# Four groups of the MLP's first layer by seven products, single modulation steps, and a schedule with other costs, in a fused hybrid block

## The chip, the core and the metric

One core of a Trainium2 chip runs the whole program. The metric is the device time of one execution in microseconds (us); the median of three runs of the kernel before is 822.44.

## What is computed

One decoder layer on x (512 tokens x 1024, fp32), with a conditioning vector c. The reference, cut to what matters here:

```python
mod = silu(c) @ w_ada + b_ada
shift1, scale1, gate1, shift2, scale2, gate2 = split(mod, 6)
h = rms_norm(x, g_pre_mix) * (1 + scale1) + shift1
z = h @ w_in                                     # GLU input | q latent | kv latent | rotary key | gates
u = silu(layer_norm(causal_depthwise_conv(ua * sigmoid(ub)), conv_norm_g, conv_norm_b))
y_a = u @ w_conv_out                             # branch A
q  = rms_norm(q_lat, q_norm_g) @ w_uq            # branch B: attention over low-rank latents
kv = rms_norm(kv_lat, kv_norm_g) @ w_ukv
y_b = softmax attention(q, kv, rope) @ w_attn_out
x = x + gate1 * rms_norm((sigmoid(g_a) * y_a + sigmoid(g_b) * y_b) @ w_out, g_post_mix)
h = rms_norm(x, g_pre_mlp) * (1 + scale2) + shift2
y = square(relu(h @ w_mlp_in)) @ w_mlp_out       # 1024 -> 4096 -> 1024
x = x + gate2 * rms_norm(y, g_post_mlp)
```

## The kernel before, in words

**Arithmetic.** Every fp32 matrix product is made of three products of the type fp32r, which rounds: `mm3` (L454) multiplies high by high, high by low and low by high part into the same PSUM bank. A high part is a ScalarE cast, a low part a VectorE subtraction (`W`, L475, for weights; `split`, L459). "A product" below is one instruction on TensorE: 128 x 128 weights times 128 x 512 (or x 256) columns.

**Who sets the order.** The program isn't issued as it is written. `Planner` (L164 to 390) records every operation with the region it reads and writes (`record`, L245; `region`, L195), gives it a cost (`cost`, L217), works back from TensorE's order when each must be done, and lists each engine's instructions by that (`plan`, L306): TensorE in the order of writing, the others by due time less a bonus (`plan.hurry`). `Arena` and `Banks` hand out places in two SBUF arenas (`f_arena` for fp32, `r_arena` for fp32r) and in PSUM. The whole is repeated `PASSES` times, each with the lifetimes of the pass before, and the pass with the shortest planned length is issued (L385), so that every instruction in the trace has the line L388. Tiles are told apart by their names: `f_arena`, `r_arena`, `psum`, `mod`, `lns` (layer norm's statistics), `stats` (those of the RMS norms).

**The front.** The tokens are loaded, normalized and transposed. The shift and scale of the first norm come from `w_ada`; they are needed as columns, one for each 128 channels. `ada_load` (L522) loads the rows of one column pair or of several, VectorE multiplies them by c and adds them up (L705 to 709), `to_columns` (L640) sums over partitions on TensorE with a vector of ones, and `first_products` (L652) forms h for these 128 channels and starts 21 products with `w_in`. The loop over `KGRP` (L694) takes channels 2 and 3 together, 4 and 5 together, then 6 and 7 singly.

**The middle.** The rest of the input projection, the latents' norm (`lat_norm`, L867), attention with the convolution spread beside it, `layer_norm` (L1233, over channels, with statistics broadcast by TensorE from diagonal matrices), the output projections and the gates.

**The MLP.** Its 4096 hidden channels are worked in four chunks (`for ch in range(NCH)`, L1527), each of eight tiles of 128 channels. A chunk's first layer takes 8 x 8 x 3 = 192 products of 512 columns (for the first four tiles of chunk 0 twice as many of 256, because the second half of the tokens comes later). The second layer (`strassen`, L1447) multiplies 2 x 2 blocks with seven products instead of eight, the sums of blocks being made by VectorE: 7 x 24 = 168 products of 512 columns. `add_block` (L1565) adds them to the result, and in the last chunk does the last norm and the output.

The core of a seven-product scheme, as it stands in the second layer:

```python
b_sub(t1, b12, b11)
b_sub(t2, b22, t1)
dve.tensor_tensor(a3(s1), A(1, 0), A(1, 1), ALU.add)
dve.tensor_tensor(a3(s2), a3(s1), A(0, 0), ALU.subtract)
product(a_form(a3(s2)), b_form(t2), ba, False)
banked(0, 1, ba)
```

The fourth argument of `product` says whether the bank is begun anew; with `False` the product is added onto what `banked` has just read out.

## Time and profile before

| | |
|---|---|
| runs | 822.37, 822.44, 826.56 us (median 822.44) |
| the profiled execution | 821.15 us; its span 819.4 us |
| TensorE busy | 799.6 us (98%), 3934 instructions, clock 0.997 of full speed |
| VectorE busy | 685.5 us (84%) |
| ScalarE busy | 423.3 us (52%) |
| GpSimd busy | 28.5 us (3%) |
| moved by DMA | 117.28 MB, mean 143 GB/s |

The span runs from the first to the last instruction of the profiled execution; its time has 1.75 us around that. Busy times are sums over the whole span and hide that the stages have different limits; the rows further down are taken by stretch.

### The profile page before, as it was taken

What the parts mean: (1) busy time and instruction counts of PE and PEld (TensorE: products, weight loads), DVE (VectorE), ACT (ScalarE), POOL (GpSimd) and SP (SyncE); (2) the same over time, 40 slices, a digit from 0 to 9 for tenths busy, and PEclk for the clock granted to TensorE, in tenths of its full rate; (3) what the DMA queues carried; (4) which work ended last, traced back from release to release, by engine and by line L of the source; (5) the groups of instructions that cost most, each with busy time, mean ns of one, the idle gap of its engine ahead of it and who ended that gap; (6) DMA issues with size and microseconds to landing.
All of it is one profiled execution on the core that took longest, in us unless ns stands there. A gap on an engine that the chain in (4) does not pass through costs nothing.

```text
span 819.4 us, 10628 instructions
## 1 busy us (share of the span) xinstructions
PE 799.6 (98%) x3934; PEld 673.5 (82%) x3934; DVE 685.5 (84%) x1014; ACT 423.3 (52%) x714; POOL 28.5 (3%) x84
## 2 busy tenths in 40 slices
PE   6999999999999999999999989999999999999995
PEld 4778988899988888888888889888888888888884
DVE  4989899999999999989999798397539993975696
ACT  5373554375894255228334496465345434553552
POOL 2001210000000000000000020000000000000001
PEclk9999999999999999999999999999999999999998
DMA  9997324202263151134799660173015831660302
GB/s 305 330 336 256 126 76 122 80 1 77 79 206 103 27 154 52 52 98 154 255 325 385 239 188 26 52 227 108 0 52 165 283 117 52 201 209 1 103 0 104
DMA packets 87111, 117.28 MB, mean 143 GB/s; under 512 B 7345, under 2 KB 61970, under 8 KB 87058
## 3 DMA queue, kind: packets, MB, share of 16 engines
q1 hardware_dynamic: 87058, 116.59, 44.1%
q8 instruction: 31, 0.51, 0.3%
q14 instruction: 22, 0.18, 0.1%
HBM read 108.18 MB, written 8.39 MB: 142 GB/s over the span
## 4 chain that ended last, share of the span: by engine, by line
PE 95%; ACT 2%; DVE 1%; POOL 1%; DMA 0%; issue 0%; DVEq 0%; ACTq 0%
PE psum L388 95%; DVE f_arena L388 1%; ACT f_arena L388 1%; POOL stats L388 1%; ACT r_arena L388 0%; DMA f_arena<-in_x_dram 0%; ACT stats L388 0%; DVEq L1639 0%; DVE mod L388 0%; ACTq L388 0%
## 5 line engine op out<-in xcount | busy, mean ns | idle before, releaser
L388 PE MATMUL psum<-r_arena 128*128 128x512 f32 (+2 forms) x3592 | 761.5, 372 | 3.2 <-ACT r_arena L388 3.1
L388 PEld LDWEIGHTS psum<-r_arena 128*128 128x128 f32 x3592 | 632.5, 188 | 114.8 <-ACT r_arena L388 3.8
L388 DVE TENSOR_TENSOR r_arena<-f_arena,r_arena 128x1024 fp32r<-128x1024 f32 (+4 forms) x234 | 247.7, 1081 | 92.1 <-PE psum L388 57.6
L388 ACT CAST r_arena<-f_arena 128x1024 fp32r<-128x1024 f32 (+4 forms) x224 | 210.2, 959 | 179.4 <-PE psum L388 117.8
L388 DVE SCALAR_TENSOR_TENSOR f_arena<-f_arena,cw 128x512 f32<-128x512 f32 x240 | 164.9, 744 | 0.0
L388 ACT ACTIVATE f_arena<-psum 128x512 f32<-128x512 f32 x64 | 38.1, 597 | 120.0 <-PE psum L388 119.8
L388 DVE TENSOR_TENSOR f_arena<-f_arena 128x1024 f32<-128x1024 f32 (+3 forms) x78 | 77.0, 1003 | 5.8 <-ACT f_arena L388 3.6
L388 ACT ACTIVATE f_arena<-f_arena 128x512 f32<-128x512 f32 (+4 forms) x100 | 58.5, 604 | 18.6 <-DVE f_arena L388 17.4
L388 DVE SCALAR_TENSOR_TENSOR f_arena<-f_arena,cT 128x256 f32<-128x256 f32 (+2 forms) x84 | 55.3, 699 | 0.1
L388 PE MATMUL psum<-ident,f_arena 128*128 128x128 f32 x234 | 34.9, 286 | 7.6 <-DVE f_arena L388 7.6
L388 PEld LDWEIGHTS psum<-ident,f_arena 128*128 128x128 f32 x234 | 28.8, 147 | 13.0 <-DVE f_arena L388 8.4
L388 DVE TENSOR_TENSOR f_arena<-psum,f_arena 128x512 f32<-128x512 f32 x52 | 35.5, 684 | 4.6 <-PE psum L388 4.4
L388 DVE TENSOR_TENSOR r_arena<-psum,r_arena 128x512 fp32r<-128x512 f32 (+2 forms) x57 | 35.7, 656 | 1.7 <-ACT r_arena L388 1.0
L388 POOL TENSOR_TENSOR stats<-stats,nhalf 128x1 f32<-128x1 f32 x24 | 20.1, 842 | 476.2 <-ACT stats L388 476.2
L388 ACT CAST r_arena<-psum 128x512 fp32r<-128x512 f32 (+2 forms) x57 | 30.1, 566 | 11.1 <-PE psum L388 10.7
L388 ACT COPY f_arena<-psum 128x512 f32<-128x512 f32 (+5 forms) x42 | 19.8, 500 | 17.6 <-PE psum L388 17.6
L388 ACT ACTIVATE r_arena<-f_arena 128x512 fp32r<-128x512 f32 (+3 forms) x20 | 13.0, 651 | 18.3 <-DVE f_arena L388 16.0
L388 DVE CUSTOM_DVE_ANT_0 f_arena<-psum,mask 128x128 f32<-128x128 f32 (+3 forms) x32 | 15.2, 485 | 2.7 <-PE psum L388 2.5
L388 ACT ACTIVATE f_arena<-f_arena,lnh 128x512 f32<-128x512 f32 x16 | 12.2, 808 | 6.8 <-DVE f_arena L388 6.7
L388 DVE TENSOR_SCALAR f_arena<-f_arena,stats 128x1024 f32<-128x1024 f32 x8 | 6.0, 751 | 10.5 <-POOL stats L388 10.5
L388 DVE SCALAR_TENSOR_TENSOR f_arena<-f_arena 128x512 f32<-128x512 f32 (+1 forms) x18 | 13.2, 743 | 0.2 <-ACT f_arena L388 0.2
L388 DVE SCALAR_TENSOR_TENSOR f_arena<-f_arena,psum 128x512 f32<-128x512 f32 x16 | 10.7, 679 | 0.0
(94 smaller groups left out, 180.3 us busy)
## 6 DMA issues: line engine op xcount, KB each, us to landing
f_arena<-in_w_ada_dram SPq DMA_DIRECT2D x16, 1024.0 KB, 5.3
f_arena<-in_w_mlp_in_dram SPq DMA_DIRECT2D x32, 512.0 KB, 4.4
f_arena<-in_w_mlp_out_dram SPq DMA_DIRECT2D x32, 512.0 KB, 5.4
f_arena<-in_w_in_dram SPq DMA_DIRECT2D x24, 512.0 KB, 4.1
f_arena<-in_x_dram SPq DMA_DIRECT2D x8, 512.0 KB, 5.4
f_arena<-in_w_ada_dram SPq DMA_DIRECT2D x16, 256.0 KB, 5.6
f_arena<-in_w_ada_dram SPq DMA_DIRECT2D x8, 512.0 KB, 7.1
h_spill<-r_arena SPq DMA_DIRECT2D x16, 256.0 KB, 3.8
```

Source lines behind the costliest of these rows:

```text
L388: getattr(self.real[o.eng], o.fn)(*o.a, **o.k)
```

## The change

1. **First MLP layer.** Four groups of four hidden tiles, `SIN` = (chunk, first tile) (0, 4), (1, 0), (1, 4), (2, 4), are worked with seven products of blocks instead of eight. A group is a product of a 512 x 1024 by a 1024 x 512 matrix; in 2 x 2 blocks a block product is 24 products of 256 columns, so 7 x 24 = 168 of 256 columns take the place of 96 of 512. `h2_sums` makes four sums of activation blocks once, `strassen_in` a group. The fp32 activations are kept for it (`h2f`, 4096 words of a partition).
2. **Front.** `KGRP` has single steps; shift and scale are summed by one VectorE instruction of 256 elements instead of two; within a step, the 21 products go by kind of part (all high by high, then high by low, then low by high). Ten small loads (six vectors, the positions, three of the convolution's weights), which stood ahead of the first step, come behind the last modulation load.
3. **`lat_norm`** takes the roots of all four token tiles in one instruction instead of eight, after all squares and before all scalings.
4. **The planner's costs** are others (a product of 256 columns, a load by the length of its pieces, a queue of eight loads, a delay for GpSimd), and 14 passes are made. So the order of instructions changes everywhere.

The diff, cut to its core (`run` gives the length in bytes of a load's contiguous pieces; `region` takes DRAM by offset):

```diff
@@ -44,10 +44,13 @@
-PASSES = 8
+SIN = ((0, 4), (1, 0), (1, 4), (2, 4))
+DEPTH = 8
+PASSES = 14
 LEAD = 15000.0
+SLOW = 4000.0
 ADAS = (1, 1, 0, 4)
-KGRP = ((2, 3), (4, 5), (6,), (7,))
+KGRP = ((2,), (3,), (4,), (5,), (6,), (7,))
...
@@ -218,17 +235,17 @@
         if fn == "dma_start":
-            return 475.0, 2000.0
+            return 375.0, 2000.0
...
-                return max(53.5, n / 2.4 + 2) * 4, 190.0
-            return max(64.0, n / 2.4 + 2.5), 190.0
+                return (213.0 if n == 1 else max(53.5, n / 2.4 + 2) * 4), 190.0
+            return max(109.0, n / 2.4 + 13.3), 190.0
...
-            o.dma = b
+            n = min(self.run(outs[0]), self.run(ins[0]), 4096)
+            o.dma = b * (13.0 + 0.0385 * n) / (16 * n)
...
                     if o.dma:
                         st = max(now + 1100.0, dma_free)
-                        dma_free = st + o.dma / 360.0
-                        o.t1 = dma_free + 910.0
+                        dma_free = st + o.dma
+                        o.t1 = dma_free + 1100.0
+                        landed.append(o.t1)
+                        free[e] = max(free[e], landed[-DEPTH])
...
@@ -660,9 +677,12 @@
-            for i in range(NA + NB):
-                o = i // 2 if i % 2 == 0 else NA + i // 2
-                mm3(pb.v(g1b[i]), w(0, o * P, P), hs(k), k == 0, k == KD - 1)
+
+            for wi, hi in ((0, 0), (0, 1), (1, 0)):
+                for i in range(NA + NB):
+                    o = i // 2 if i % 2 == 0 else NA + i // 2
+                    pe.matmul(pb.v(g1b[i]), lhsT=w(0, o * P, P)[wi], rhs=hs(k)[hi], start=k == 0 and wi + hi == 0,
+                              stop=k == KD - 1 and wi == 1)
...
             for j in range(KD):
-                for s in range(2):
-                    if j == 0:
-                        dve.tensor_scalar(accv[:, s], av[:, s, 0], cT[:, 0:1], None, ALU.mult)
-                    else:
-                        dve.scalar_tensor_tensor(accv[:, s], av[:, s, j], cT[:, j:j + 1], accv[:, s], op0=ALU.mult, op1=ALU.add)
+                if j == 0:
+                    dve.tensor_scalar(accv, av[:, :, 0], cT[:, 0:1], None, ALU.mult)
+                else:
+                    dve.scalar_tensor_tensor(accv, av[:, :, j], cT[:, j:j + 1], accv, op0=ALU.mult, op1=ALU.add)
...
@@ -719,6 +739,17 @@
+        plan.after = ada_end
+        row_loads(1, ("gpl", g_pre_mlp), ("cb", conv_b), ("cng", conv_norm_g), ("cnb", conv_norm_b),
+                  ("qg", q_norm_g), ("kvg", kv_norm_g))
+        sp.dma_start(out=pos4, in_=positions[0].rearrange("(a p) -> a p", p=P))
...
+            sp.dma_start(out=fa.v(cwr)[at:at + r1 - r0, c0:c0 + P], in_=cw_rows[r0:r1])
+        plan.after = None
...
@@ -865,16 +896,19 @@
-                rstd(s[:, 2:3], s[:, 0:1], 1.0 / QL)
-                rstd(s[:, 3:4], s[:, 1:2], 1.0 / KL)
...
+            rstd(s[:, 2 * NT:], s[:, :2 * NT], 1.0)
...
@@ -1524,11 +1561,110 @@
+        def h2_sums():
+
+            Y = {(j, i): k4(fa.v(h2f[j]))[:, :, 256 * i:256 * i + 256] for j in range(2) for i in range(2)}
+            for nm, o, a, b in ((3, (0, 1), (1, 1), (0, 1)), (1, (0, 0), None, (0, 0)), (2, (1, 1), (1, 1), (0, 0)),
+                                (4, (1, 0), (1, 0), (1, 1))):
+                if nm == 1:
+
+                    dve.tensor_tensor(Y[0, 0], Y[1, 1], Y[0, 0], ALU.subtract)
+                    dve.tensor_tensor(Y[0, 0], Y[0, 0], Y[0, 1], ALU.subtract)
+                else:
+                    dve.tensor_tensor(Y[o], Y[a], Y[b], ALU.subtract)
+                hl = pair(1024)
+                act.copy(k4(ra.v(hl[0])), Y[o])
+                dve.tensor_tensor(k4(ra.v(hl[1])), Y[o], k4(rf(hl[0])), ALU.subtract)
+                h2s_[nm] = hl
+            fa.free(*h2f)
+
+        def strassen_in(hv, n0, c0):
...
+            def product(xb, y, b, first):
+                w = W(fa.v(xb, "p (k n) -> p k n", k=4), 4, 256)
...
+                for m in range(2):
+                    for k in range(4):
+                        mm3(pb.v(b)[:, m * 256:(m + 1) * 256], w(k, m * P, P), ys_[k], first and m == 0 and k == 0, k == 3,
+                            skip_group_check=True)
+                w.free()
...
+            def keep(i, n, b):
+                act.copy(o(i, n), ps(b))
+
+            def done(i, n, b):
+                v = o(i, n)
+                dve.tensor_tensor(v, ps(b), v, ALU.add)
+                act.activation(v, v, AF.Relu)
+                act.activation(v, v, AF.Square)
+
+            x11, x12 = x_(0, 0), x_(0, 1)
+            ba, bb, bc_ = (pb.alloc() for _ in range(3))
+            product(x11, (0, 0), ba, True)
+            keep(0, 0, ba)
+            product(x12, (1, 0), bc_, True)
+            done(0, 0, bc_)
+            pb.free(bc_)
+            x21, x22 = x_(1, 0), x_(1, 1)
+            s1, s2 = fa.alloc(1024), fa.alloc(1024)
+            sub(s1, x21, x22, ALU.add)
+            sub(s2, s1, x11)
+            product(s2, 2, ba, False)
+            keep(0, 1, ba)
+            product(s1, 1, bb, True)
+            fa.free(s1)
+            keep(1, 1, bb)
+            sub(x21, x11, x21)
+            fa.free(x11)
+            product(x21, 3, ba, False)
+            fa.free(x21)
+            done(1, 1, ba)
+            sub(x12, x12, s2)
+            fa.free(s2)
+            product(x12, (1, 1), bb, False)
+            fa.free(x12)
+            done(0, 1, bb)
+            pb.free(bb)
+            product(x22, 4, ba, False)
...
             for n0 in range(0, HPC, GRP):
+                if (ch, n0 - n0 % 4) in SIN:
+                    if n0 % 4 == 0:
+                        if not h2s_:
+                            h2_sums()
+                        strassen_in(hv, n0, (ch * HPC + n0) * P)
...
+                    continue
```

How the order moves, at the three places that the prediction speaks of. In these rows `x` with a number counts equal instructions in a row.

TensorE in the MLP, from the last transposes into it to the end, before (`ident` marks a transpose, `onesr` a broadcast of the last gate):

```order
L388 MATMUL psum<-ident,f_arena 128x128 x12
L388 MATMUL psum<-r_arena 128x512 x11
L388 MATMUL psum<-r_arena 128x256 x6
L388 MATMUL psum<-ident,f_arena 128x128 x4
L388 MATMUL psum<-r_arena 128x256 x63
L388 MATMUL psum<-ident,f_arena 128x128 x12
L388 MATMUL psum<-r_arena 128x256 x123
L388 MATMUL psum<-r_arena 128x512 x1176
L388 MATMUL psum<-r_arena,onesr 128x512 x4
L388 MATMUL psum<-r_arena 128x512 x168
```

and now:

```order
L410 MATMUL psum<-ident,f_arena 128x128 x12
L410 MATMUL psum<-r_arena 128x512 x17
L410 MATMUL psum<-r_arena 128x256 x24
L410 MATMUL psum<-ident,f_arena 128x128 x4
L410 MATMUL psum<-r_arena 128x256 x53
L410 MATMUL psum<-ident,f_arena 128x128 x12
L410 MATMUL psum<-r_arena 128x256 x283
L410 MATMUL psum<-r_arena 128x512 x168
L410 MATMUL psum<-r_arena 128x256 x336
L410 MATMUL psum<-r_arena 128x512 x264
L410 MATMUL psum<-r_arena 128x256 x168
L410 MATMUL psum<-r_arena 128x512 x360
L410 MATMUL psum<-r_arena,onesr 128x512 x4
L410 MATMUL psum<-r_arena 128x512 x168
```

In all 384 products of 512 columns have gone and 672 of 256 have come, in three pieces; ahead of the first four transposes stand 17 + 24 products instead of 11 + 6.

TensorE in the front, from the first modulation column to the last (`ones` 128x1 is the sum over partitions for a shift and a scale), before:

```order
L388 MATMUL psum<-ones,f_arena 128x1 x2
L388 MATMUL psum<-r_arena 128x512 x49
L388 MATMUL psum<-ones,f_arena 128x1 x2
L388 MATMUL psum<-r_arena 128x512 x8
L388 MATMUL psum<-ones,f_arena 128x1 x2
L388 MATMUL psum<-r_arena 128x512 x9
L388 MATMUL psum<-ones,f_arena 128x1 x2
L388 MATMUL psum<-r_arena 128x512 x20
L388 MATMUL psum<-ones,f_arena 128x1
L388 MATMUL psum<-r_arena 128x512
L388 MATMUL psum<-ones,f_arena 128x1
L388 MATMUL psum<-r_arena 128x512 x54
```

and now:

```order
L410 MATMUL psum<-ones,f_arena 128x1 x2
L410 MATMUL psum<-r_arena 128x512 x23
L410 MATMUL psum<-ones,f_arena 128x1 x2
L410 MATMUL psum<-r_arena 128x512 x22
L410 MATMUL psum<-ones,f_arena 128x1 x2
L410 MATMUL psum<-r_arena 128x512 x21
L410 MATMUL psum<-ones,f_arena 128x1 x2
L410 MATMUL psum<-r_arena 128x512 x21
L410 MATMUL psum<-ones,f_arena 128x1 x2
L410 MATMUL psum<-r_arena 128x512 x21
L410 MATMUL psum<-ones,f_arena 128x1 x2
L410 MATMUL psum<-r_arena 128x512 x27
```

The sums of the pair (4, 5), the two instructions x2 after x49 and after x8, and those of 6 and 7 are now asked for one by one, 21 to 23 products apart.

VectorE at the layer norm, from the last token tile's statistics to the diagonals (`lns` 128x4 are the small sums, 128x512 the additions of convolution taps), before:

```order
L388 TENSOR_TENSOR lns<-lns 128x4
L388 SCALAR_TENSOR_TENSOR f_arena<-f_arena 128x512
L388 TENSOR_SCALAR lns<-lns 128x4
L388 TENSOR_TENSOR lns<-lns 128x4
L388 SCALAR_TENSOR_TENSOR f_arena<-f_arena 128x512
L388 TENSOR_SCALAR lns<-lns 128x4
L388 TENSOR_TENSOR lns<-lns 128x4 x2
L388 SCALAR_TENSOR_TENSOR f_arena<-f_arena 128x512
L388 TENSOR_TENSOR lns<-lns 128x4
L388 SCALAR_TENSOR_TENSOR f_arena<-f_arena 128x512
L388 TENSOR_SCALAR f_arena<-f_arena,cT 128x1024
L388 TENSOR_SCALAR f_arena<-ident,lns 128x128
L388 TENSOR_TENSOR lns<-lns 128x4
L388 TENSOR_SCALAR f_arena<-ident,lns 128x128 x3
```

and now:

```order
L410 TENSOR_TENSOR lns<-lns 128x4
L410 SCALAR_TENSOR_TENSOR f_arena<-f_arena 128x512
L410 TENSOR_SCALAR lns<-lns 128x4
L410 TENSOR_TENSOR lns<-lns 128x4 x2
L410 TENSOR_SCALAR lns<-lns 128x4
L410 TENSOR_TENSOR lns<-lns 128x4 x2
L410 TENSOR_SCALAR f_arena<-ident,lns 128x128
L410 TENSOR_TENSOR lns<-lns 128x4
L410 TENSOR_SCALAR f_arena<-ident,lns 128x128 x3
```

One addition of 512 elements stands among the small sums instead of four, and one of 1024 ahead of the first diagonal is gone. On TensorE the broadcast (`f_arena,ones`) had 27 products of 512 columns ahead of it since the last transposes, and has 16 now.

## Rows read from the trace of the kernel before

**Rows 1.** The head of the profile page: the span, and busy time (share of the span, instructions) of each engine.

```profile
span 819.4 us, 10628 instructions
...
PE 799.6 (98%) x3934; PEld 673.5 (82%) x3934; DVE 685.5 (84%) x1014; ACT 423.3 (52%) x714; POOL 28.5 (3%) x84
```

**Rows 2.** The chain of work that ended last, in order of time: start us, us, engine and what it worked on.

```profile
44.81 197.30 PE psum L388 x1131
...
242.77 190.97 PE psum L388 x866
...
481.39 329.38 PE psum L388 x1545
```

**Rows 3.** TensorE's timeline in two stretches that hold one kind of product alone: start us, us from the first start to the last end, engine, line, operation, tiles, shape, count.

```profile
490.72 13.48 PE L388 MATMUL psum<-r_arena 128*128 128x256 f32 x111
...
649.64 22.60 PE L388 MATMUL psum<-r_arena 128*128 128x512 f32 x99
```

**Rows 4.** Groups of instructions by form over the whole span: count | busy us, mean ns of one | idle time before them and what ended it.

```profile
L388 PE MATMUL psum<-r_arena 128*128 128x512 f32 x2866 | 665.9, 391 | 1.5 <-ACT r_arena L388 1.5
...
L388 PE MATMUL psum<-r_arena 128*128 128x256 f32 x418 | 55.2, 285 | 1.7 <-ACT r_arena L388 1.6
```

**Rows 5.** Busy time by stretch: the MLP from its start to the end of the third chunk, then the second layers of chunks 0, 1 and 2. Columns: stretch, length, busy us (instructions) of PE, PEld, DVE, ACT, POOL, granted clock, DMA share, GB/s.

```profile
481.40:728.30 246.90, 246.90 (x1183) 208.48 (x1184) 182.55 (x185) 133.96 (x171) 1.38 (x1) 1.00 0.40 127
526.70:564.90 38.20, 38.20 (x171) 31.61 (x170) 34.11 (x33) 27.09 (x32) 0.00 (x0) 1.00 0.66 206
608.50:646.60 38.10, 38.10 (x170) 31.55 (x169) 35.69 (x38) 23.66 (x24) 0.00 (x0) 1.00 0.59 188
690.20:728.30 38.10, 38.10 (x170) 31.54 (x169) 36.85 (x39) 23.97 (x25) 0.00 (x0) 1.00 0.63 197
```

**Rows 6.** Groups by form from 526.7 to 564.9 us (a second layer): the low part of 1024 elements, a sum of blocks, the addition of a PSUM result, the cast, the copy out of PSUM.

```profile
L388 DVE TENSOR_TENSOR r_arena<-f_arena,r_arena 128x1024 fp32r<-128x1024 f32 x23 | 27.4, 1220 | 4.7 <-PE psum L388 3.2 <-ACT f_arena L388 1.0
L388 ACT CAST r_arena<-f_arena 128x1024 fp32r<-128x1024 f32 x23 | 23.6, 1053 | 8.8 <-PE psum L388 6.5 <-issue 1.9 <-DVE f_arena L388 0.2
L388 DVE TENSOR_TENSOR f_arena<-f_arena 128x1024 f32<-128x1024 f32 x4 | 4.9, 1219 | 0.3 <-ACT f_arena L388 0.3
L388 DVE TENSOR_TENSOR f_arena<-psum,f_arena 128x512 f32<-128x512 f32 x6 | 4.1, 686 | 0.5 <-PE psum L388 0.5
L388 ACT COPY f_arena<-psum 128x512 f32<-128x512 f32 x7 | 4.1, 581 | 1.9 <-PE psum L388 1.9
```

**Rows 7.** VectorE's timeline in a second layer: two low parts without a gap.

```profile
631.25 2.35 DVE L388 TENSOR_TENSOR r_arena<-f_arena,r_arena 128x1024 fp32r<-128x1024 f32 x2
```

**Rows 8.** Busy time by stretch in the attention stage, with the columns of rows 5.

```profile
260.00:300.00 40.00, 40.00 (x178) 33.14 (x177) 38.94 (x52) 14.32 (x18) 0.00 (x0) 1.00 0.32 92
300.00:340.00 40.00, 40.00 (x189) 32.97 (x189) 40.00 (x59) 20.91 (x47) 0.00 (x0) 1.00 0.10 27
```

**Rows 9.** The timeline near 43 us: in brackets the engine's idle time before, and what ended it.

```profile
43.03 0.50 PE L388 MATMUL psum<-ones,f_arena 128*128 128x1 f32 x4
...
44.81 1.45 PE L388 MATMUL psum<-r_arena 128*128 128x512 f32 x5 [1.28 <-ACT r_arena L388]
```

**Rows 10.** Busy time of the first 20 us, with the columns of rows 5.

```profile
0.00:20.00 20.00, 12.81 (x63) 8.06 (x64) 8.12 (x17) 11.97 (x23) 5.98 (x50) 1.00 0.99 304
```

**Rows 11.** The timeline at the layer norm's broadcast (the last row): the last transposes, the cover, VectorE's last square, GpSimd's root, the first diagonal.

```profile
359.38 0.38 PE L388 MATMUL psum<-ident,f_arena 128*128 128x128 f32 x2
...
359.52 6.42 PE L388 MATMUL psum<-r_arena 128*128 128x512 f32 x27
...
360.40 0.43 DVE L388 CUSTOM_DVE_ANT_0 f_arena<-f_arena 128x256 f32<-128x256 f32 x1
...
363.22 1.41 POOL L388 TENSOR_TENSOR lns<-lns,nhalf 128x4 f32<-128x4 f32 x1 [253.92 <-DVE lns L388]
...
364.67 0.29 DVE L388 TENSOR_SCALAR f_arena<-ident,lns 128x128 f32<-128x128 f32 x1 [0.25 <-POOL lns L388]
...
365.78 0.39 PE L388 MATMUL psum<-f_arena,ones 128*128 128x128 f32 x2
```

**Rows 12.** The timeline on the way into the MLP: transposes, the last products of the output projection and the first of the MLP, and ScalarE's work between.

```profile
473.46 1.53 PE L388 MATMUL psum<-ident,f_arena 128*128 128x128 f32 x12 [0.25 <-DVE f_arena L388]
...
474.75 3.12 PE L388 MATMUL psum<-r_arena 128*128 128x512 f32 x14
...
477.18 1.07 ACT L388 ACTIVATE f_arena<-f_arena 128x1024 f32<-128x1024 f32 x1
...
478.22 0.61 ACT L388 ACTIVATE f_arena<-psum 128x512 f32<-128x512 f32 x1
...
478.98 0.42 ACT L388 CAST r_arena<-f_arena 128x256 fp32r<-128x256 f32 x1
...
479.45 0.96 PE L388 MATMUL psum<-r_arena 128*128 128x256 f32 x3 [1.58 <-ACT r_arena L388]
...
480.57 0.66 PE L388 MATMUL psum<-ident,f_arena 128*128 128x128 f32 x4 [0.16 <-DVE f_arena L388]
```

**Rows 13.** The timeline after the last product: VectorE's addition of it, its next work, and GpSimd's last root.

```profile
810.80 0.69 DVE L388 TENSOR_TENSOR f_arena<-psum,f_arena 128x512 f32<-128x512 f32 x1 [0.90 <-PE psum L388]
...
811.41 0.68 DVE L388 TENSOR_TENSOR f_arena<-f_arena 128x512 f32<-128x512 f32 x1
...
812.65 0.55 POOL L388 TENSOR_TENSOR stats<-stats,nhalf 128x1 f32<-128x1 f32 x1 [1.04 <-ACT stats L388]
```

More of the change, by code (lines that the diff above doesn't have):

```diff
@@ L182, in __init__ @@
         self.after = None
+        self.slack = 0.0
     class Engine:
@@ L208, in region, with run @@
         return name, range(lo // u, hi // u + 1)
+    @staticmethod
+    def run(ap):
+        dims = [list(d) for d in ap.ap]
+        if ap.tensor.name.split("_bitcast")[0].endswith("arena") or dims[0][0] == 0:
+            dims = dims[1:]
+        n = 1
+        for s, c in reversed(dims):
+            if s != n:
+                break
+            n *= c
+        return 4 * n
     @staticmethod
@@ L1406, in emit @@
                 h2[:] = [pair(T) for _ in range(KD)]
+                h2f[:] = [fa.alloc(4 * T) for _ in range(2)]
             hsl = slice(tp * 256, (tp + 1) * 256)
@@ L1531, in emit @@
             for n0 in range(0, HPC, GRP):
+                if (ch, n0 - n0 % 4) in SIN:
[3 more added lines that the diff above has]
+                        strassen_in(hv, n0, (ch * HPC + n0) * P)
+                        if ch >= NCH - 2:
+                            take(late, 2 * ADAS[1])
+                        if (ch, n0) == SIN[-1]:
+                            for nm in list(h2s_):
+                                ra.free(*h2s_.pop(nm))
+                    continue
                 bs = [pb.alloc() for _ in range(GRP)]
```

80 lines of the change are left out of this document (52 added, 28 removed).

## The prediction

> **What bounds the kernel now.** I read the head of the profile page first: TensorE is busy for 799.6 of 819.4 us [rows 1]. Then the chain of waits: it runs on TensorE almost throughout; its three longest pieces are 44.8 to 242.1, 242.8 to 433.7 and 481.4 to 810.8 us [rows 2], and the detours between them are short. From 481.4 us to the last product it never leaves TensorE. So time is won in two ways only: fewer or shorter matmuls, or fewer detours. VectorE is the second engine (685.5 us), and it decides how much can be loaded onto it.
>
> The prices of a matmul come from two pure stretches of TensorE's timeline [rows 3]. 99 products of 512 columns take 22.60 us; the last one shows its own duration, 0.39 us by the groups [rows 4], so one starts every (22.60 - 0.39)/98 = 0.2266 us. 111 of 256 columns take 13.48 us: (13.48 - 0.29)/110 = 0.1199 us each [rows 3, 4]. Half the columns cost 53%, not 50%.
>
> **The change part by part.** The sum is made against the profiled execution's own 821.15 us (span 819.4). The median of the three runs shown is 822.44, 1.3 above it.
>
> *Four groups of the MLP's first layer by seven products.* The order shows it: 4 x 96 = 384 products of 512 columns go, 4 x 168 = 672 of 256 columns come. 384 x 0.2266 = 87.0 us, 672 x 0.1199 = 80.6 us: **-6.4 us**, all of it on the path, because TensorE waits nowhere in that stretch. In both stretches every product has a weight load of its own. The Trainium skill, "TensorE: Matmul & The Clock Gate", section "Back-to-back issue gap", speaks against the change: for a stream of weight loads and matmuls it gives some 81 ns at 128 columns and 131 ns at 512; 256 would lie near 98 on the line between, and the term would be 672 x 97.7 - 384 x 131 ns = +15.3 us, an estimate. Its formula for a single matmul, N/2.4 + 2.5 ns, would give 384 x 215.8 - 672 x 109.2 ns = -9.5 us, an estimate too. The rows show 226.6 and 119.9 ns in just such streams, so both are set aside and the sum goes by the rows.
>
> *What VectorE pays for that.* Between 481.4 and 728.3 us, which holds all four groups, VectorE is busy 182.55 of 246.9 us [rows 5]. A group now splits 7 blocks instead of 4 (3 more low parts), forms 4 sums of blocks, and adds 3 PSUM results to kept ones: 7 x 1.22 + 3 x 0.69 = 10.6 us by the durations [rows 6], x 4 = 42.4. The sums of the activations, made once, are 5 subtractions and 4 low parts: 9 x 1.22 = 11.0. That makes 236 us of work in 246.9 - 6.4 = 240.5 us: 98%. Back to back the same instructions start 1.13 us apart (2.35 us for two [rows 7]), not 1.22, so the true load is nearer 92%. Can VectorE run so full without making TensorE wait? From 260 to 340 us it is busy 38.94 and 40.00 of 40 us, and TensorE is busy 40.00 of 40 in both [rows 8]. So I expect the planned order to hold, and charge **+0.5 us**; bounds 0 (it hides) and +12.6 (rivals).
> ScalarE gets 3 more casts (1.05 us each) and copies of 0.58 us per group [rows 6]; with 134 of 246.9 us busy [rows 5] it has room: nothing. The weight blocks are the same bytes in pieces of the same length, and the DMA share of that stretch is 0.40: nothing; if the arena, which now holds 4096 words of activations longer, delayed one load, its landing shows as a wait of ScalarE.
>
> *The front.* The pairs of modulation columns (2,3) and (4,5) are loaded and summed one by one, and each step sums shift and scale in one instruction. Before, the sums of the pair (4,5) end late: TensorE finishes the column sums at 43.5 us, and the next product waits for ScalarE until 44.81, 1.28 us [rows 9]. The new order asks for one column pair's sums every 21 to 23 products (4.8 to 5.2 us) and has them 6 to 9 products ahead of their use, so this wait should go: **-1.3 us**. What is late next is the load: 1.51 MB per step (8 x 512 B rows per partition of 1.05 MB, and 0.46 MB of weights). At the rate of the first 20 us, 304 GB/s [rows 10], that is 5.0 us per step against 4.8 of products; all 14.2 MB would be there at about 47 us, and the last sums are asked for only after 141 products, at about 57 us. So it is covered by some 8 us. The small loads that move behind the last modulation load (ten, on SP's queue) free slots there; their readers, transposes and copies, stand behind the last of these sums, ten microseconds after the last modulation load. Bounds: -1.8 (some of the restarts go as well), +3 if pieces of 512 B move at four fifths of the rate.
> In the products of a step the order is now all high parts first, then the others: the same 21 instructions, nothing.
>
> *The latents' norm* takes its square roots in one POOL instruction for all four token tiles instead of eight. The transposes that wait for it stand behind 96 products (21.8 us) on TensorE; the path is POOL's root, 1.41 us for a joint one [rows 11], and four token tiles squared and scaled, 640 elements each, 8 x 0.7 us by ScalarE's 1.07 us for 1024 [rows 12]: 7 us, and 12 with a fixed part for each of the 16 instructions. Nothing; without that cover the joint wait would cost about 4.
>
> *Layer norm: less cover.* The last transposes end near 359.7 us, 27 products of 0.227 us (6.1 us) follow, and the broadcast of the statistics starts at 365.78 without a wait [rows 11]. Now 16 products stand there (3.6 us). The path under them: ScalarE's sum and VectorE's square to 360.83, the small sums with four 512-element products between them, POOL's root 363.22 to 364.63, the diagonals at 364.67. In the new order only one of those four remains between the small sums, so the path shrinks by 3 x 0.6 = 1.8 us, from about 5.6 to about 3.8, and the ScalarE diagonals add 0.4 to 1.3. TensorE would wait 0.6 to 2.0 us: **+1.5 us**. Bounds 0 and +3.
>
> *Into the MLP (473 to 481 us).* TensorE works, waits 1.58 us for a cast of the first activations, then again 0.16, and runs its first products slowly [rows 12]; of 6.6 us from 474.75 on, 11 + 7 products and 4 transposes fill 3.8, so 2.8 are lost, and 0.25 before. ScalarE had put a square of 1024 and one of 512 ahead of that cast. Now three casts come before those squares, and 17 products instead of 11 cover them; but the 24 that follow want all eight columns, and the last four casts still stand behind the squares: I get 2.3 us lost. **-0.7 us**, bounds -2.9 and +1.
>
> *The tail.* After the last product VectorE adds it (810.80), then works on the third token tile before the fourth [rows 13]. In the new order the third tile's gate product stands ahead of that addition: one instruction of 0.6 us less: **-0.6 us**, and not more, since the fourth tile's root ends at 813.2. Bounds -0.7 and 0.
>
> Sum: -6.4 + 0.5 - 1.3 + 1.5 - 0.7 - 0.6 = **-7.0 us**: 814.2 us in terms of the profiled execution, and 1.3 more, **815.4 us**, in terms of the median.
>
> **The rivals.**
> *All the waits go* (as in the second half before). For it: VectorE ran the middle of the kernel at 97 to 100% without a wait of TensorE [rows 8]. Then -6.4 - 1.8 - 2.9 - 0.7 = -11.8: 810.6 us.
> *A wait in PSUM takes the place of the product saved.* Three of a group's seven products add onto a bank that must first be copied or read out; if each finds that copy just starting, it waits for its 0.58 us [rows 6]: 12 x 0.58 = 7.0 us, 6.5 beyond my +0.5: 821.9, no change that can be told. Against it: a product of the other bank (2.9 us) lies between in two cases of three.
> *VectorE becomes the bound of the MLP: slower.* It needs 236 us there. If it reaches only the share of the three second-layer stretches, (34.11 + 35.69 + 36.85)/114.4 = 93.2% [rows 5], the stretch takes 253.1 us instead of 240.5: +12.6, so 815.4 + 12.1 = 827.5. It decides from a share of 93.5% down. For it: those stretches are the fullest of the MLP and the work added is of their kind. Against it: [rows 8], and that durations count overlapping ends twice.
>
> **How the numbers follow.** A measurement of this kernel tells 0.5% (4.1 us) from no change. Forecast 0.64 (its own terms: 811.5 to 818.3), all waits gone 0.15, PSUM 0.13, VectorE 0.08. Faster by over 0.5% (below 818.3): 0.64 + 0.15 = 0.79; within: 0.13; slower (above 826.6): 0.08. The range reaches from just below the second case to the third: 809.5 to 822.0, and leaves out 0.08 and the ends. That the change does not do what it says is excluded for the matmuls by the order.
>
> **What would show it.** Right: TensorE's stretch from the first 256-column product to the last product 6 to 7 us shorter, with 672 more starts 0.120 us apart; no wait at 43 us; a wait of 1 to 2 us at the layer norm's broadcast; VectorE busy at 90 to 98% from 481 to 720 us. Wrong: TensorE waiting for VectorE's low parts or for ScalarE's copies inside the new groups, waits for modulation loads before 60 us, or 256-column products further apart than 0.12 us.

## The result, and the profile after

The changed kernel took 814.88 us (median of 814.60, 814.88 and 815.82) against 822.44: a ratio of 0.9899, 95% interval 0.9871 to 0.9926. Run again beside 17 runs of the kernel before it took 815.11 (6 runs) against 823.03: 0.9903, 0.9881 to 0.9925. So it is about 7.6 to 7.9 us faster; 815.4 was forecast. The profiled executions are closer together than that, 815.82 against 821.15: the one was the longest of its three runs, the other shorter than all three of its own. The second profile of the kernel before, below, shows what such a difference is made of.

The head of the page after, with the columns of [rows 1]: 288 products more, and 3.1 us less of a busy TensorE; VectorE has gone from 84% to 90%.

```profile
span 814.0 us, 11293 instructions
...
PE 796.5 (98%) x4222; PEld 681.1 (84%) x4222; DVE 732.2 (90%) x1049; ACT 441.6 (54%) x735; POOL 22.0 (3%) x77
```

The chain of waits after, as in [rows 2]. Behind 497 us it is one piece of TensorE to the last gate. But the piece that ran from 44.8 to 242.1 us ends at 183 us now: from there to 245 us the chain goes to and fro between TensorE and VectorE.

```profile
61.20 121.92 PE psum L410 x667
183.15 1.84 DVE r_arena L410 x3
185.80 2.95 DVE f_arena L410 x11
...
197.86 6.19 DVE f_arena L410 x14
...
245.29 118.00 PE psum L410 x534
...
369.09 92.57 PE psum L410 x423
...
497.33 301.09 PE psum L410 x1680
```

TensorE's timeline in two stretches of one kind of product, as in [rows 3]. (26.43 - 0.28)/218 = 0.1200 us for 256 columns, (32.69 - 0.39)/142 = 0.2275 for 512 (134 of them elsewhere: 30.54 us, 0.2267 each): the prices of before.

```profile
498.74 26.43 PE L410 MATMUL psum<-r_arena 128*128 128x256 f32 x219
...
607.67 32.69 PE L410 MATMUL psum<-r_arena 128*128 128x512 f32 x143
...
735.66 30.54 PE L410 MATMUL psum<-r_arena 128*128 128x512 f32 x134
```

For the stages I read from the traces when TensorE starts its first product of 512 columns, when it starts the one behind the front's 168, when it starts the first product of the MLP (the first of 256 columns there) and the last of all, and when the span ends. Lengths in us:

| profile | first product at | front | to the MLP | MLP | end | span |
|---|---|---|---|---|---|---|
| before | 21.63 | 43.66 | 412.06 | 333.02 | 9.00 | 819.4 |
| before, again | 23.32 | 43.66 | 412.02 | 334.27 | 9.00 | 822.3 |
| changed | 23.36 | 43.00 | 413.94 | 325.88 | 7.82 | 814.0 |
| changed, again | 22.82 | 43.01 | 414.56 | 325.90 | 7.88 | 814.2 |

The MLP gives 7.1 to 8.4 us, front and end 0.65 and 1.1 to 1.2; on the way to the MLP 1.9 to 2.5 are lost. In the first pair the first product also starts 1.73 us later.

### The profile page after: what moved, and what is told of

Same layout as the page of the kernel before. It is cut to its first block, busy times and chain, and to the rows that moved or that the text cites. A ratio compares the mean times of both kernels' runs of the same rounds, so it can differ in the third digit from the quotient of the medians.

```text
span 814.0 us, 11293 instructions
## 1 busy us (share of the span) xinstructions
PE 796.5 (98%) x4222; PEld 681.1 (84%) x4222; DVE 732.2 (90%) x1049; ACT 441.6 (54%) x735; POOL 22.0 (3%) x77
## 3 DMA queue, kind: packets, MB, share of 16 engines
HBM read 108.18 MB, written 8.39 MB: 143 GB/s over the span
## 4 chain that ended last, share of the span: by engine, by line
PE 84%; DVE 8%; ACT 3%; DMA 2%; issue 1%; POOL 1%; SPq 0%; DVEq 0%
PE psum L410 84%; DVE f_arena L410 5%; DVE r_arena L410 3%; ACT f_arena L410 2%; ACT r_arena L410 1%; DMA c<-in_c_dram 1%; DMA f_arena<-in_w_in_dram 1%; POOL stats L410 1%; ACT stats L410 0%; SPq L410 0%; DMA rows<-in_kv_norm_g_dram 0%; DVE mod L410 0%; DVEq L1775 0%; DVEq L410 0%
## 5 line engine op out<-in xcount | busy, mean ns | idle before, releaser
L410 PE MATMUL psum<-r_arena 128*128 128x512 f32 (+3 forms) x3880 | 756.4, 355 | 0.9 <-ACT r_arena L410 0.6
L410 PEld LDWEIGHTS psum<-r_arena 128*128 128x128 f32 x3880 | 640.1, 189 | 100.7 <-ACT r_arena L410 2.6
L410 ACT CAST r_arena<-f_arena 128x1024 fp32r<-128x1024 f32 (+4 forms) x240 | 224.9, 964 | 169.1 <-PE psum L410 115.3
L410 DVE TENSOR_TENSOR r_arena<-f_arena,r_arena 128x1024 fp32r<-128x1024 f32 (+4 forms) x250 | 265.9, 1089 | 31.2 <-PE psum L410 21.4
L410 DVE TENSOR_TENSOR f_arena<-f_arena 128x1024 f32<-128x1024 f32 (+3 forms) x99 | 102.3, 1047 | 3.0 <-ACT r_arena L410 1.6
L410 ACT ACTIVATE f_arena<-f_arena 128x512 f32<-128x512 f32 (+4 forms) x112 | 66.1, 606 | 29.0 <-DVE f_arena L410 27.9
L410 ACT ACTIVATE f_arena<-psum 128x512 f32<-128x512 f32 x52 | 30.6, 594 | 71.9 <-PE psum L410 71.3
L410 DVE SCALAR_TENSOR_TENSOR f_arena<-f_arena,cT 128x256 f32<-128x256 f32 (+1 forms) x70 | 56.0, 801 | 7.4 <-DMA f_arena<-in_w_ada_dram 6.4
L410 DVE TENSOR_TENSOR f_arena<-psum,f_arena 128x512 f32<-128x512 f32 x64 | 42.9, 681 | 6.8 <-PE psum L410 6.8
L410 POOL TENSOR_TENSOR stats<-stats,nhalf 128x1 f32<-128x1 f32 (+1 forms) x17 | 13.3, 785 | 471.2 <-ACT stats L410 471.1
L410 ACT ACTIVATE r_arena<-f_arena 128x512 fp32r<-128x512 f32 (+3 forms) x20 | 13.0, 651 | 18.0 <-DVE f_arena L410 15.4
L410 DVE CUSTOM_DVE_ANT_0 f_arena<-psum,mask 128x128 f32<-128x128 f32 (+3 forms) x32 | 14.8, 481 | 0.1
L410 DVE SCALAR_TENSOR_TENSOR f_arena<-f_arena 128x512 f32<-128x512 f32 (+1 forms) x18 | 13.2, 740 | 0.0
```

What stands on the lines that cost most here:

```text
L410: getattr(self.real[o.eng], o.fn)(*o.a, **o.k)
```

## Experiments

All run on one core; "changed kernel" is the one above. Where no order is pinned the planner makes its schedule anew. The runs fall into four groups on four chips; beside them the kernel before had medians of 823.03 to 824.33, so between groups a difference of about 1 us tells nothing. `after_again`, `no_groups`, `groups_only` and `old_costs` ran on one chip.

**The changed kernel and the kernel before once more** (no edit).

> The changed kernel once more, to know how far one profiled execution may lie from another. Both theories: 814.9 us, within 1 us; ratio to the kernel before 0.989 to 0.992. If the extra time at the front (first product at 23.4 us instead of 21.6) and in the attention stage belongs to the order and not to this one execution, it shows again: first product at 23.1 to 23.6 us, layer norm's broadcast at 368 to 369.5 us.

815.11 us (814.13 to 815.94). The longer middle of the changed kernel shows again (the broadcast at 369.18 us); the first product comes at 22.82, ahead of the 23.1 to 23.6 expected. Whether its lateness belongs to the change, the kernel before tells:

> The kernel before once more with a profile. Its runs spread from 820.3 to 827.4 us, those of the changed kernel from 814.1 to 815.9, and its profiled execution was one of its shortest. Theory: TensorE's start varies by 1 to 2 us from run to run (first product at 21.6 in two profiles of this order), and the kernel before, whose VectorE has some 15 us to spare up to the layer norm, passes such a delay on to the end, while the changed kernel takes it up in attention. Then this profile shows 822 to 826 us with the first product or the front's end later by as much as the time, and the stages behind as long as in the first profile. Rival, the spread arises elsewhere: a longer stage behind the front.

824.04 us; the other runs of the kernel before on that chip had a median of 824.26. Its first product starts at 23.32 too. The rows are TensorE's start in this profile (in brackets the wait and what ended it): the load of c comes 0.8 us late, and then the 16 passes of the first modulation products take 4.25 us, the first three starts 382 to 427 ns apart, the next 257 and the rest 216 (3.61 us in the first profile of the kernel before, all 216 ns apart).

```profile
9.93 0.27 PE L388 MATMUL psum<-ident,c 8*128 8x8 f32 x1 [0.79 <-DMA c<-in_c_dram]
...
13.57 4.25 PE L388 MATMUL psum<-f_arena,cT 128*1 128x256 f32 x16
...
23.32 0.97 PE L388 MATMUL psum<-r_arena 128*128 128x512 f32 x3
```

Up to the MLP this delay of 1.69 us is passed on whole (front and middle are as long as in the first profile to 0.04 us), and at the MLP 1.25 us come on top, told below. Half of the theory holds: the start varies from run to run. That the changed kernel takes it up in attention does not: in its order the stretch from the front's end to the layer norm's broadcast is 302.3 to 303.6 us in six profiles (300.5 in both of the kernel before, with as many instructions of TensorE), and where the first product started at 21.69 (`five_b`), the broadcast came at 367.27 instead of 368.9 to 369.4.

**Without the groups, and the groups alone.**

```diff
-SIN = ((0, 4), (1, 0), (1, 4), (2, 4))
+SIN = ()
...
```

> The changed kernel without the four seven-product groups (they are worked as the others, with 96 products of 512 columns each; the planner makes its schedule anew). Theory of the sum: the groups are worth 6.4 us and VectorE's extra work costs 0 to 0.5, so this is 5.9 to 6.4 us slower than the changed kernel: 820.8 to 821.4 us. Rival, VectorE eats the groups' gain and the new schedule is what helps: no more than 3 us slower, 815 to 818.

822.17 us (12 runs, 820.48 to 823.55), 7.1 slower than the changed kernel (the cut part of the edit gives up the storage that the groups need). Its MLP takes 332.53 us, 6.63 more; every other stage is within 0.7 us.

```diff
 # the kernel before
+SIN = ((0, 4), (1, 0), (1, 4), (2, 4))
...
+                if (ch, n0 - n0 % 4) in SIN:
+                    if n0 % 4 == 0:
...
+                        strassen_in(hv, n0, (ch * HPC + n0) * P)
```

> The kernel before with the four seven-product groups alone (old planner costs, old pairs of modulation columns, old norms). Theory of the sum: 6.4 us less, up to 0.5 back: 816.0 to 816.5 us. Rival, the groups gain only with the corrected costs (a planner that thinks a product of 256 columns takes 109 ns puts VectorE's work late, and TensorE waits): 818 to 822.

818.82 us (818.03 to 819.21): 4.2 less than the kernel before, between the theories. The MLP takes 326.24 us, 6.78 less than before: that part of the sum holds without the new costs. Both lengths hold the waits at the MLP's start too, which differ. Behind the last transposes TensorE waits in neither trace: there `groups_only` takes 315.55 us for 809 products of 256 columns and 964 of 512, the kernel before 320.21 for 123 and 1348. That is 4.66 us less, and by the two prices it should be 4.76. But the way to the MLP is 3.66 us longer, in one place. TensorE's timeline there, and the windows around it (stretch, length, busy us of PE, PEld, DVE, ACT, POOL, granted clock, DMA share, GB/s):

```profile
480.99 0.80 PE L389 MATMUL psum<-r_arena 128*128 128x256 f32 x2 [4.05 <-ACT f_arena L389]
481.59 0.84 PE L389 MATMUL psum<-ident,f_arena 128*128 128x128 f32 x3
482.08 2.27 PE L389 MATMUL psum<-r_arena 128*128 128x256 f32 x9
```

```profile
476.00:481.00 5.00, 0.95 (x9) 0.64 (x7) 4.44 (x7) 4.39 (x13) 1.38 (x2) 0.84 0.30 111
481.00:486.00 5.00, 5.00 (x23) 5.00 (x24) 4.97 (x9) 4.81 (x13) 0.12 (x1) 0.50 0.86 297
```

TensorE waits 4.05 us for ScalarE, and in the 5 us behind that the granted clock is 0.50, the lower of its two levels (1.2 GHz): products of 256 columns start 213 ns apart instead of 120 (from 486.4 us on they are 120 apart again). The Trainium skill, "TensorE: Matmul & The Clock Gate", section "HAM oscillation — how this bites in real kernels", says that a wait between two bursts can put the clock back to half rate; the row agrees, with 0.50. The kernel before shows it both ways: in the first profile it waits 1.58 us there and the clock stays at 1.00; in the second it waits 1.59 us and the next 5 us have 0.66.

```profile
476.00:481.00 5.00, 3.52 (x20) 2.87 (x18) 4.74 (x6) 4.01 (x12) 0.16 (x1) 1.00 0.66 216
481.00:486.00 5.00, 4.65 (x22) 4.25 (x23) 4.84 (x9) 5.00 (x14) 1.21 (x2) 0.66 0.84 251
```

In the changed kernel TensorE is busy through it, 5.00 and 4.76 of 5 us, at 1.00:

```profile
476.00:481.00 5.00, 5.00 (x29) 4.30 (x28) 4.74 (x10) 5.00 (x13) 0.00 (x0) 1.00 0.78 267
481.00:486.00 5.00, 4.76 (x39) 4.44 (x38) 3.99 (x6) 5.00 (x13) 1.63 (x2) 1.00 0.74 248
```

**The planner's costs**, all of them back, those of loads, those of engines.

```diff
-            return max(109.0, n / 2.4 + 13.3), 190.0    # old_costs, old_engine
+            return max(64.0, n / 2.4 + 2.5), 190.0
...
-            o.dma = b * (13.0 + 0.0385 * n) / (16 * n)  # old_costs, old_dma
+            o.dma = b
```

> The changed kernel with the planner's costs of the kernel before; all other edits stay. Theory that the new costs lost time ahead of the MLP (five transposes more ahead of the first modulation products: 1.2 to 1.7 us; attention paced by VectorE: 1 to 2 us) and that the rest doesn't need them: 2 to 3 us faster than the changed kernel, 812 to 813, first product at 21.4 to 21.9 us. Rival, the corrected costs are needed by the groups and the layer norm: slower than the changed kernel by 1 to 5 us, 816 to 820.

> The changed kernel with the planner's model of loads as before (no queue of eight, one rate for all lengths), the costs of the engines as corrected. With all costs old, 1.3 us were lost, the sum of a loss of 4 us on the way into the MLP and a gain of 2.4 us in attention. Theory that the model of loads brings the gain into the MLP (weights are asked for late enough and early enough): 816 to 819 us, a wait of 3 us or more at the MLP's first products. Rival, the costs of the engines bring it: 813 to 815.5, no such wait.

> The mirror: costs of TensorE's products and of ScalarE's sine as before, the model of loads as corrected. Theory that the model of loads brings the gain on the way into the MLP: 813 to 815.5 us. Rival, the costs of the engines bring it (a product of 512 columns planned at 215.8 instead of 226.6 ns makes the planner think that TensorE arrives 20 us earlier at the MLP than it does): 816 to 819, with a wait of 3 us or more there.

816.40 us (6 runs), 817.59 (6) and 823.20 (12). With all costs old it is 1.3 us slower, at the lower end of the rival's range; the first product came at 23.69, though five transposes fewer stand ahead of it, so the theory fell; its half about attention holds, as the windows further down show. The other two are not the halves of the first: each of the three is another schedule. With the engines' costs old TensorE waits 2.87 us at 386 us and 2.47 at the MLP's first products, with a granted clock of 0.52 in the 5 us from 486 us: the corrected costs of the engines bring the smooth way into the MLP, as the rival had it, and the loss without them is larger than its 816 to 819. With `old_dma` TensorE has no wait there above 0.5 us, and yet some 2.5 us are lost, which neither theory had: 1.2 of them by a longer front (44.21 us) and 0.7 in the MLP.

**Five transposes of the start moved back by hand**, all else as in the changed kernel's own order.

```diff
+        for n, o in enumerate(pe[m - 5:m]):
+            key[o.i] = key[pe[m + 7].i] + 0.1 * (n + 1)
```

> The changed kernel's own order with one piece moved by hand: the eight first modulation products stand ahead of the last 5 of the 14 transposes before them (as in the kernel before); everything else keeps its order. Theory that these transposes hold up the front: first product 1.1 to 1.3 us earlier (21.6 to 22.2 us), the front's end and all that follows as much earlier: 813.8 us. Rival, the modulation products wait for c or for their load anyway: no change, 815. Second rival, the front gains but the attention stage gives it back, because VectorE, 74.69 of 75 us busy there, paces TensorE: first product 1.2 us earlier, layer norm's broadcast at 369 us all the same, 815.

815.34 us (5 runs): no change. The first product starts at 24.14, the latest of all. TensorE reaches the modulation products at 13.01 us, but they take 4.71 us (five starts 383 to 427 ns apart, one of 300, then 216), against 3.82 in the changed kernel, which begins them at 14.20. In this profile, in `before_again`, `five_groups` and the changed kernel's first they fall to 216 between 14.8 and 15.4 us, in `old_dma` already at 13.5 and in `old_costs` only at 15.9; in eight of the fourteen profiles all are 216 apart. So the theory that the transposes hold up the front falls, and the later first product need not be the change's: with the same order of these instructions `five_b` starts it at 21.69, as early as the kernel before. The factor of two looks like TensorE's lower clock, but the granted clock is 1.00 from 13.0 to 15.5 us in the trace: that stays open.

**The late modulation sums behind the layer norm.**

```diff
-        take(late, ADAS[3])
         plan.boost = 3000
         layer_norm()
         plan.boost = 0
+        plan.after = ln_end[0]
+        take(late, ADAS[3])
+        plan.after = None
```

> The changed kernel with one due time more: the first eight late modulation sums (1024 elements, 1.27 us each on VectorE, not needed before the output projection) may not run before the layer norm's small sums; the planner makes its schedule anew. In the changed kernel they stand ahead of the layer norm (one stood there in the kernel before), in a stretch where VectorE is busy 295 of 298 us (70 to 368 us; 283.5 in the kernel before). Theory that VectorE paces TensorE there: the layer norm comes earlier among TensorE's products, and the waits ahead of the broadcast (6.6 to 7.4 us of lost time up to it, 4.0 in the kernel before) fall by 2 to 3 us: 812 to 813 us. Rival, those waits are in the attention stage between 200 and 250 us and have nothing to do with these sums: 814.5 to 815.5. Second rival, the sums come too late now for the gate and the way into the MLP: 816 or more.

814.89 us (814.15 to 815.73): not to be told from the changed kernel. The broadcast comes 50 products earlier; the way to the MLP takes 413.53 us, which tells nothing either (413.94 and 414.56 in the changed kernel's profiles, 413.49 in `front_first`). The waits between 200 and 250 us stay, so the first rival is right about most of the loss. The windows there, of the kernel before, the changed kernel and `old_engine`: from the first to the second VectorE's busy time goes from 70.47 to 74.69 of 75 us, TensorE's from 74.65 to 74.50, and the instructions that TensorE starts from 481 to 478.

```profile
170.00:245.00 75.00, 74.65 (x481) 67.67 (x481) 70.47 (x175) 56.29 (x135) 0.00 (x0) 1.00 0.32 98
```

```profile
170.00:245.00 75.00, 74.50 (x478) 66.70 (x476) 74.69 (x181) 56.13 (x133) 0.00 (x0) 1.00 0.32 99
```

```profile
170.00:245.00 75.00, 74.65 (x481) 67.87 (x480) 70.47 (x174) 56.74 (x135) 0.00 (x0) 1.00 0.32 99
```

The third shows that the loss there comes with the new costs of the engines, not with the other edits. From the first to the last of attention's 58 products of 384 columns TensorE starts 482 instructions. The eight profiles that have the changed kernel's order there take 76.68 to 76.79 us for them, with VectorE busy 76.4 to 76.5. `old_costs` and `old_engine`, with all other edits in, take 75.50 and 75.53 us for as many in another order, with VectorE busy 71.5 and 71.2.

**More groups:** all seven that begin with all tokens at hand; or one more, the first or the second of chunk 3.

```diff
-SIN = ((0, 4), (1, 0), (1, 4), (2, 4))
+SIN = ((0, 4), (1, 0), (1, 4), (2, 0), (2, 4), (3, 0), (3, 4))  # all_groups
+SIN = ((0, 4), (1, 0), (1, 4), (2, 4), (3, 0))                  # five_groups
+SIN = ((0, 4), (1, 0), (1, 4), (2, 4), (3, 4))                  # five_b
```

> Seven-product groups in all seven places of the MLP's first layer that begin with all tokens at hand, instead of four (chunk 2's first, chunk 3's two are added). Theory of the sum: 3 x (96 x 0.2266 - 168 x 0.1199) = 3 x 1.61 = 4.8 us less: 810.3. Rival, VectorE is the bound: it is busy 243.5 of the 275.1 us between the MLP's last transposes and the last gate, 3 x 10.6 = 32 us more make 275.5 in 270.3; if durations count fully, TensorE waits some 5 us: 815, and more if chunk 3's gate sums come on top (817).

821.39 us (12 runs): some 6 slower than with four groups (6.0 against `front_first`, which ran on the same chip), as in the rival, and worse. Most of the 4.8 us is eaten by TensorE's waits for low parts in chunk 2's second layer, and the end grows from 7.8 to 13.2 us, because VectorE, busy all 46 us from 760 to 806, still has five products with the gate (512 elements each) and all eight final sums to do behind the last product. The window, and TensorE's rows in it:

```profile
690.00:728.00 38.00, 35.20 (x163) 28.12 (x163) 38.00 (x39) 19.38 (x20) 0.00 (x0) 1.00 0.35 111
```

```profile
696.60 0.73 PE L410 MATMUL psum<-r_arena 128*128 128x512 f32 x2 [0.45 <-ACT r_arena L410]
697.82 10.78 PE L410 MATMUL psum<-r_arena 128*128 128x512 f32 x46 [0.49 <-DVE r_arena L410]
710.38 0.98 PE L410 MATMUL psum<-r_arena 128*128 128x512 f32 x3 [1.78 <-DVE r_arena L410]
```

> The changed kernel with one seven-product group more, the first of chunk 3 (tiles 0 to 3). Seven groups cost VectorE its slack in chunk 2's second layer (busy 38.00 of 38 us between 690 and 728, TensorE 35.20) and lengthened the end. Theory that VectorE's room decides group by group: in chunk 3's first layer it is busy 23.3 of 39 us, 10.6 more fit: 1.6 us less, 813.5. Rival, VectorE comes out of chunk 2's second layer already late (38.00 of 38 busy there in the changed kernel too, without a wait), so that the group's sums come late and TensorE waits for them, 1 to 3 us: 815 to 816.5.

> The same with the other group of chunk 3 (tiles 4 to 7) in its place, half of the first layer later. Theory that VectorE's room decides: 813.5, as with the first group. Rival that VectorE is late from chunk 2's second layer: this group has 22 us to recover in, so it gains the 1.6 us (813.5) where the first doesn't. Second rival, the last gate's sums and the second layer's blocks collide with it: the last product or the tail comes later, 815 to 818.

814.60 us (813.28 to 815.82), between theory and rival, and 817.92 (816.69 to 818.27), as in the second rival. Both MLPs are shorter, 324.86 and 324.44 against 325.90, so 1.0 and 1.5 of the 1.6 us come. The first keeps its 1.0 us and may be 0.3 to 0.5 us better than the changed kernel, which its runs can't tell. The second loses more than its gain at the end (12.05 us): VectorE's rows behind its last product. The final sums of all four token tiles, 5.38 us, are still to do. In the changed kernel, the rows below them, the last such piece takes 1.41 us.

```profile
803.35 0.68 DVE L410 TENSOR_TENSOR f_arena<-psum,f_arena 128x512 f32<-128x512 f32 x1
803.95 1.89 DVE L410 TENSOR_TENSOR f_arena<-f_arena 128x512 f32<-128x512 f32 x3
805.75 5.38 DVE L410 SCALAR_TENSOR_TENSOR f_arena<-f_arena,stats 128x512 f32<-128x512 f32 x8
```

```profile
809.00 0.68 DVE L410 TENSOR_TENSOR f_arena<-f_arena 128x512 f32<-128x512 f32 x1
809.60 1.41 DVE L410 SCALAR_TENSOR_TENSOR f_arena<-f_arena,stats 128x512 f32<-128x512 f32 x2
```

## Why the prediction was right, step by step

**Four groups, -6.4: right**, and the one term that carries the result. Two pairs of kernels measure it with what VectorE pays and with the waits at the MLP's start: -6.63 (`no_groups`) and -6.78 (`groups_only`). Where TensorE does not wait the two prices are right to 0.1 us of 4.76, as worked out at `groups_only`.

**VectorE's load, +0.5: nothing is paid.** From 480.3 to 724 us VectorE is busy 226.3 of 243.7 us, 93%, where I had worked out 98% by durations and 92% by starts. The window's row, with the columns of [rows 5]:

```profile
480.30:724.00 243.70, 242.94 (x1482) 218.10 (x1481) 226.32 (x230) 158.91 (x207) 2.91 (x3) 1.00 0.41 132
```

With four groups TensorE has no wait from 497 us to the last product. The rival of VectorE as the bound was wrong for this change and right in kind: `all_groups` shows it three groups further on.

**The front, -1.3: -0.65.** The wait of 1.28 us [rows 9] is gone; TensorE now goes on 0.36 us after the column sums begin.

```profile
42.97 0.50 PE L410 MATMUL psum<-ones,f_arena 128*128 128x1 f32 x4
43.33 5.18 PE L410 MATMUL psum<-r_arena 128*128 128x512 f32 x21
48.35 0.50 PE L410 MATMUL psum<-ones,f_arena 128*128 128x1 f32 x4
```

Half of it is given back in small pieces: a step takes 5.38 us from one column sum to the next, where 21 products and the sums at their price take 4.76 + 0.36. Over the front the column sums take 1.34 us less of TensorE's time from start to start (2.17 instead of 3.51), but the same 168 products take 0.69 more (40.13 instead of 39.44). The sum had the products of a step at nothing, as the same 21 instructions in another order. Whether their order or the single steps cost this, no run separates. No load is late.

**Layer norm, +1.5: mis-sized, and the loss was elsewhere.** The broadcast behind its 16 products starts at 369.09; from the last transposes [rows 11] it took 6.40 us with 27 products (6.12), now 4.26 with 16 (3.63): 0.35 us more lost. The wait of 1 to 2 us that I named as a sign isn't there. GpSimd's root took 1.02 us, not 1.41.

```profile
364.83 0.44 PE L410 MATMUL psum<-ident,f_arena 128*128 128x128 f32 x2
...
365.03 3.92 PE L410 MATMUL psum<-r_arena 128*128 128x512 f32 x16
...
367.65 1.02 POOL L410 TENSOR_TENSOR lns<-lns,nhalf 128x4 f32<-128x4 f32 x1 [258.75 <-DVE lns L410]
...
369.09 1.17 PE L410 MATMUL psum<-f_arena,ones 128*128 128x128 f32 x8
```

Just ahead of these transposes TensorE loses time as well, and for that the sum had no term. The longest such wait of the changed kernel's two profiles is in the second; the kernel before has none there:

```profile
362.36 0.63 PE L410 MATMUL psum<-ident,f_arena 128*128 128x128 f32 x4 [0.45 <-DVE f_arena L410]
```

The whole middle lost 1.9 to 2.5 us. Some 1.4 of it goes between 160 and 262 us, in attention (an estimate from the trace: the starts of TensorE's instructions there against the usual distance of their kind). The sum had no term for attention: I had taken from [rows 8] that a full VectorE costs TensorE nothing. From 260 to 340 us it costs nothing; between 170 and 245 us, where the chain of waits goes to and fro, TensorE loses time beside a full VectorE, nearly all of it in pieces too small to show as waits. The longest wait, now and, below it, at the same place before:

```profile
245.29 1.12 PE L410 MATMUL psum<-f_arena 128*128 128x512 f32 x2 [0.53 <-ACT f_arena L410]
```

```profile
242.77 1.77 PE L388 MATMUL psum<-f_arena 128*128 128x512 f32 x4 [0.35 <-ACT f_arena L388]
```

That VectorE's fuller order causes the loss is the likeliest reading of the three windows above, and not shown: the runs with the old costs of the engines have another order of TensorE there too, and no run has taken work from VectorE in that stretch alone.

**Into the MLP, -0.7: about right against the first profile, too small against the second.** The wait of 1.58 us [rows 12] is gone (32 products run without a break from 476.33 us), and waits of 0.24, 0.22 and 0.30 us have come:

```profile
476.33 5.93 PE L410 MATMUL psum<-r_arena 128*128 128x512 f32 x32
...
484.42 6.37 PE L410 MATMUL psum<-r_arena 128*128 128x256 f32 x51 [0.24 <-DVE f_arena L410]
491.01 1.53 PE L410 MATMUL psum<-ident,f_arena 128*128 128x128 f32 x12 [0.22 <-DVE f_arena L410]
...
497.33 2.88 PE L410 MATMUL psum<-r_arena 128*128 128x256 f32 x22 [0.30 <-ACT r_arena L410]
```

Against the first profile of before the MLP gained 7.14 us, 0.5 more than the groups alone; against the second 8.39, 1.8 more, since there the clock had fallen and products of 256 columns started 213 ns apart from 483.4 to 485.8 us. The term that I missed is the clock behind this wait.

**The tail, -0.6: -1.1 to -1.2**, outside its bounds. The end is 7.82 and 7.88 us, 9.00 before. VectorE's part is as forecast: from the start of the last addition to the end of the last scaling it now takes 3.93 us (807.08 to 811.01), and took 4.54 ([rows 13], 810.80 to 815.34), one instruction less.

```profile
807.08 0.68 DVE L410 TENSOR_TENSOR f_arena<-psum,f_arena 128x512 f32<-128x512 f32 x1
807.68 1.40 DVE L410 SCALAR_TENSOR_TENSOR f_arena<-f_arena,stats 128x512 f32<-128x512 f32 x2
```

```profile
813.93 1.41 DVE L388 SCALAR_TENSOR_TENSOR f_arena<-f_arena,stats 128x512 f32<-128x512 f32 x2
```

That addition starts 0.5 us later behind the last product than before, so this gain is nearly used up. The rest is behind the last scaling, where the last of the output is still to be moved: 3.0 us to the end of the span instead of 4.0. The sum had no term for that, and why it is shorter stays open.

So the sum in terms of the profiles, -7.0, stands between -5.3 (the first pair) and -8.1 (the second). The gains were too small in the tail and, where the clock had fallen, into the MLP, and too large in the front; of the losses that I charged, VectorE's was not paid and layer norm's was a quarter of its size at the broadcast. Against that stand a loss in attention and, in the first pair, a first product 1.73 us later, which the sum did not have. That the forecast of 815.4 is within 0.6 us of the medians is luck in part: these cancel, and I had set the changed kernel's median 1.3 us above its profile, where it lay 0.8 to 0.9 below.

## What to carry to other kernels

Where one engine is the bound, a change that shortens its own instructions is worth their count times the pitch (the distance of two starts) read from a pure stretch of the timeline (here to 0.4 us of 6.4), as long as the second engine can take the added work. Here VectorE was busy 93% of the stretch and nothing was lost; three groups more cost some 6 us instead of gaining 4.8, and a fifth group kept its gain at one place and lost it at another. What a re-planned order does beside that is of the size of the smaller terms: four sets of costs for the same edits gave 815.1 to 823.2 us, and the slowest had a wait of 2.47 us at the entry to a stage, with a granted clock of 0.52 in the 5 us from 486 us. One profile of a kernel is not its median: look at a second before explaining 2 us.

## What the runs showed of the hardware that was not expected

The same wait of TensorE, 1.58 and 1.59 us in the same program, was followed once by a granted clock of 1.00 and once by 0.66 over the next 5 us; after 4.05 us it was 0.50, and products of 256 columns started 213 ns apart. The first modulation products started 216 or 427 ns apart at 13 us into the program, with the granted clock shown as 1.00 both times; the first product came between 21.6 and 23.0 us in the eight profiles in which all were 216 ns apart, and between 22.4 and 24.1 in the other six. And 128 x 512 products started 226.7 ns apart in one stretch of the changed kernel and 227.5 in another.
